# Seven of the sixteen blocks of an MLP's down projection by Strassen's seven products

## The chip, the core and the metric

The kernel runs on one core of one Trainium2 chip. The time is the device time of one launch in microseconds (us), the median of several runs. The engines have short names: PE is TensorE, ACT is ScalarE, DVE is VectorE, POOL is GpSimd and SP is SyncE, which issues the loads.

## What is computed

Two layers of a decoder trunk act on 256 tokens of width 1024 in float32. Each layer is a mixing part (attention, a recurrent branch and a pooling branch) and then an MLP. Only the MLP changes:

```python
h = h + RMSNorm_post(mix)
h = h + RMSNorm_post(SquaredReLU-MLP(RMSNorm_pre(h)))
```

The MLP's up projection is [256 x 1024] by [1024 x 4096], its hidden values are relu(.)^2, and its down projection is [256 x 4096] by [4096 x 1024].

## The kernel before

**A product in three matmuls.** Every float32 operand is split into two parts that TensorE takes as `float32r`: ACT copies the value rounded (the "hi", line 84) and DVE subtracts it from the original (the "lo", line 85). A product of two operands is then hi by hi, hi by lo and lo by hi, three matmuls that accumulate in one bank of PSUM (`mm3`, lines 91 to 94).

**The weights.** They come as 316 units of 128 x 1024 floats (512 KB), in the order in which they are used. SP issues one load for each (line 134) into one of 4 buffers named `raw`. ACT makes `wh` of it and DVE `wl`, into 8 buffers each. `take(n)` hands out the next n units, `split_to` and `ahead` issue copies and subtractions for units that come later, `load_to` issues loads. A raw buffer is free for the next load when DVE's subtraction has read it. The units on either side of a change of stage are split in two halves of 512 columns (`fine`).

**The MLP.** The 4096 hidden rows go in 8 chunks of 512. One *up unit* makes 256 hidden rows for all tokens: 48 matmuls of 256 columns into one bank (`w_unit`, line 276). Then ACT applies Relu out of the bank (line 731), squares (line 732) and copies the hi (line 84), and DVE subtracts the lo. The names in the profile are `z` for these values and `hid` for their two parts; `mh` and `ml` are the parts of the MLP's input. A chunk's share of the down projection is 48 matmuls of 512 columns (`s_hu`, line 289), which add to four banks: two halves of the tokens by two halves of the columns. All 8 chunks add to the same four banks (all banks are named `ps`). The loop, lines 745 to 750, puts the up units of the next chunk ahead of the down projection of this one. The first chunk (`up_first`, line 698) is computed with tokens as rows, since the second half of the tokens isn't normalised yet; eight transposes (line 706) turn it, one up unit later.

**The end of a layer.** The last two chunks' down projection goes half by half of the tokens (lines 750 to 770). After each half follows `residual` (line 253): ACT sums the squares of a bank (`junk`, line 229), DVE multiplies the bank by a gain (`yg`, line 264), DVE adds the two sums (line 233), ACT takes the root (line 245), DVE the reciprocal (line 246), and DVE adds to `h` (line 269). Then `mix_norm` does the same for the next layer's norm and scales (`un`, line 315), PE transposes (line 216), and ACT and DVE make `uh` and `ul` of the result (lines 222 and 224). The next layer's first products follow on PE (line 303). Both norm helpers are issued with a higher priority, so a scheduler moves them up on their engines. Each engine runs its own list of instructions in order.

Of the kernel before, what the change touches and what calls it, by code (L numbers as in the profile page):

```python
# [9 lines left out]
F32 = mybir.dt.float32  # L10
# [6 lines left out]
L = 2  # L17
D = 1024
# [16 lines left out]
FINE = (8, 8)  # L35
SQRT_2_PI = 0.7978845608028654
# [16 lines left out]
def trunk(ctx, tc, x, wts, rgw, par, gpost, eye, ctab, out):  # L53
    nc = tc.nc
    V, A, PE = nc.vector, nc.scalar, nc.tensor
# [23 lines left out]
    def bank(shape, nm="ps"):  # L79
        return psum.tile(shape, F32, tag="b", name=nm)  # L80
# [253 lines left out]
    for l in range(L):  # L334
# [358 lines left out]
        yb = [[bank([P, 512]) for _ in range(2)] for _ in range(2)]  # L693

        def new_hidden():
            return (acts.tile([P, 2, 4, T], F32R, tag="hi", name="hid"))

        def up_first():
            hus = take(4)
            hid = new_hidden()  # L700
            zs = []

            def hidden_T(tt):
                p2 = bank([P, 4, P])
                for j in range(4):
                    PE.transpose(p2[:, j, :], zs[tt][:, j * P:(j + 1) * P], ident)
                split(hid[:, 0, :, tt * P:(tt + 1) * P], hid[:, 1, :, tt * P:(tt + 1) * P], p2[:])

            for tt in range(2):
# [6 lines left out]
                z = ttile([P, 512], nm="z")  # L716
                A.activation(z[:], ps[:], AF.Relu)
                V.tensor_tensor(out=z[:], in0=z[:], in1=z[:], op=ALU.mult)
                zs.append(z)
            later(1, lambda: hidden_T(0))  # L720
            later(1, lambda: hidden_T(1))
            ahead()
            return hid

        def up(fc):
            hid = new_hidden()
            for u in range(2):
                ps = w_unit(take(2), uh, ul)
                tick()
                z = ttile([P, 2, T], nm="z")  # L730
                A.activation(z[:], ps[:], AF.Relu)
                A.activation(z[:], z[:], AF.Square)
                split(hid[:, 0, 2 * u:2 * u + 2, :], hid[:, 1, 2 * u:2 * u + 2, :], z[:])
                ahead()
            return hid

        def down(fc, hid):
            for nh in range(2):
                for i in range(2):
                    hu, = take(1)  # L740
                    for tt in range(2):
                        s_hu(yb[tt][nh][:], hu, hid[:, 0], hid[:, 1], 2 * i, tt, fc == 0 and i == 0, False)
                    ahead()

        hid = up_first()
        for fc in range(1, 7):
            nxt = up(fc)
            down(fc - 1, hid)
            hid = nxt
        hids = [hid, up(7)]  # L750
        hus = take(8)
# [3 lines left out]
        for tt in range(2):  # L755
            for f in range(2):
                for nh in range(2):
                    for i in range(2):
                        if tt == 1 and f == 1 and nh == 1 and i == 0 and l + 1 < L:
                            mix_features(0, un[0], l + 1)  # L760
                        s_hu(yb[tt][nh][:], hus[4 * f + 2 * nh + i], hids[f][:, 0], hids[f][:, 1], 2 * i, tt,
                             False, f == 1 and i == 1)
            residual(tt, yb[tt], msq[tt], gB)
# [43 lines left out]
def _layout(i):  # L807
    qc = np.concatenate([np.arange(hd * 64, hd * 64 + 64) for hd in _HEADS])
    units, rg, par, gp = [], [], [], []
    for l in range(L):  # L810
# [17 lines left out]
        up = _w_units(i["w_mlp_up"][l]).reshape(8, 4, P, HU_COLS)  # L828
        dn = _s_units(i["w_mlp_down"][l]).reshape(2, 8, 2, P, HU_COLS).transpose(1, 0, 2, 3, 4).reshape(8, 4, P, HU_COLS)
        units.append(up[0])  # L830
        for f in range(1, 8):
            units.append(up[f])
            units.append(dn[f - 1])
        units.append(dn[7])
# [34 lines left out]
```

## Time and profile before

| | |
|---|---|
| runs | 964.25, 965.38 and 965.0 us, median 965.0 |
| profiled execution | 964.16 us, its span 962.3 us, granted PE clock 0.999 |
| matmul instructions of PE | 5628, and 88 others in PE's row |
| loads of weight units | 316 of 512 KB |

The span runs from the first to the last instruction of the profiled execution; 1.9 us of its time lie around the span. A row of the timeline has the start in us, the duration of one instruction (or of a run of equal ones), engine, line and operation, then the tile written and the tiles read, the shape, and in brackets how long the engine was idle before it and what it waited for. On PE the matmuls are pipelined: one of 512 columns is shown as 0.39 us long, and the next one starts before it ends.

### The profile page before, as it was taken

The numbers are of one execution on the slowest core, as the hardware profiler recorded it, in microseconds if no ns is written. First come the engines' busy times: TensorE is split into PE (matmuls) and PEld (weight loads), VectorE is DVE, ScalarE is ACT, GpSimd is POOL, SyncE is SP. The second block draws the span as 40 slices with busy tenths as digits, with TensorE's granted clock in tenths as the row PEclk, the third lists the DMA queues.
The fourth block names the chain that finished last, engine by engine and source line by source line (L and its number), as shares of the span: only waits on it lengthen the run. The fifth ranks groups of instructions, "written<-read, shape, count | busy, mean of one in ns | idle before, by whom it ended". The sixth has DMA issues, their size and how long they took to land.

```text
span 962.3 us, 14953 instructions
## 1 busy us (share of the span) xinstructions
PE 951.3 (99%) x5716; PEld 835.3 (87%) x5716; DVE 649.7 (68%) x1101; ACT 599.8 (62%) x1001; POOL 2.6 (0%) x20
## 2 busy tenths in 40 slices
PE   8999999999999999999999999999999999999997
PEld 5898988988888999999888989888888899999995
DVE  6877886779768645445586778777897585545542
ACT  7754864789737655455566657566895476555541
POOL 0000000000000000000000000000000000000000
PEclk9999999999999999999999999999999999999999
DMA  7765456453755766665457536536358285665631
GB/s 277 244 205 185 132 166 195 161 178 111 254 161 176 226 192 192 183 192 176 134 183 257 172 111 210 179 103 219 124 178 262 88 276 179 195 185 188 185 122 44
DMA packets 48743, 173.28 MB, mean 180 GB/s; under 512 B 5408, under 2 KB 5792, under 8 KB 48672
## 3 DMA queue, kind: packets, MB, share of 16 engines
q1 hardware_dynamic: 48384, 172.16, 55.4%
q8 instruction: 45, 0.74, 0.3%
q14 instruction: 26, 0.21, 0.1%
q10 hardware_dynamic: 288, 0.17, 0.1%
HBM read 171.26 MB, written 1.05 MB: 179 GB/s over the span
## 4 chain that ended last, share of the span: by engine, by line
PE 97%; DMA 1%; ACT 1%; DVE 1%; issue 0%; SPq 0%; DVEq 0%; ACTq 0%
PE ps L92 28%; PE ps L93 28%; PE ps L94 28%; PE ps L303 8%; PE ps L391 1%; PE ps L439 1%; PE ps L428 1%; DMA raw<-wts 1%; PE ps L216 1%; PE ps L371 0%; PE ps L619 0%; ACT wh L84 0%; DVE h L269 0%; ACT junk L229 0%; DVE wl L85 0%
## 5 line engine op out<-in xcount | busy, mean ns | idle before, releaser
L85 DVE TENSOR_TENSOR wl<-raw,wh 128x1024 fp32r<-128x1024 f32 (+1 forms) x348 | 385.7, 1123 | 189.1 <-ACT wh L84 180.4
L84 ACT ACTIVATE wh<-raw 128x1024 fp32r<-128x1024 f32 (+1 forms) x348 | 334.2, 986 | 242.6 <-PE ps L94 106.2
L92 PE MATMUL ps<-mh,wh 128*128 128x256 f32 x448 | 126.9, 283 | 0.0
L94 PE MATMUL ps<-mh,wl 128*128 128x256 f32 x448 | 126.8, 283 | 0.0
L93 PE MATMUL ps<-ml,wh 128*128 128x256 f32 x448 | 126.8, 283 | 0.0
L92 PE MATMUL ps<-uh,wh 128*128 128x256 f32 x384 | 109.0, 284 | 0.0
L93 PE MATMUL ps<-ul,wh 128*128 128x256 f32 x384 | 108.7, 283 | 0.0
L94 PE MATMUL ps<-uh,wl 128*128 128x256 f32 x384 | 108.6, 283 | 0.0
L93 PE MATMUL ps<-wl,hid 128*128 128x512 f32 x256 | 99.9, 390 | 0.0
L92 PE MATMUL ps<-wh,hid 128*128 128x512 f32 x256 | 99.8, 390 | 0.0
L94 PE MATMUL ps<-wh,hid 128*128 128x512 f32 x256 | 99.6, 389 | 0.0
L92 PEld LDWEIGHTS ps<-mh,wh 128*128 128x128 f32 x448 | 86.0, 192 | 0.5
L93 PEld LDWEIGHTS ps<-ml,wh 128*128 128x128 f32 x448 | 85.9, 192 | 0.5
L94 PEld LDWEIGHTS ps<-mh,wl 128*128 128x128 f32 x448 | 86.0, 192 | 0.0
L92 PE MATMUL ps<-wh,uh 128*128 128x512 f32 x200 | 79.2, 396 | 0.7 <-ACT uh L222 0.7
L94 PE MATMUL ps<-wh,ul 128*128 128x512 f32 x200 | 78.1, 390 | 0.4 <-DVE ul L224 0.4
L93 PE MATMUL ps<-wl,uh 128*128 128x512 f32 x200 | 78.1, 390 | 0.0
L92 PEld LDWEIGHTS ps<-uh,wh 128*128 128x128 f32 x384 | 73.6, 192 | 1.1 <-issue 0.7
L93 PEld LDWEIGHTS ps<-ul,wh 128*128 128x128 f32 x384 | 73.6, 192 | 0.4
L94 PEld LDWEIGHTS ps<-uh,wl 128*128 128x128 f32 x384 | 73.6, 192 | 0.0
L94 PEld LDWEIGHTS ps<-wh,hid 128*128 128x128 f32 x256 | 48.1, 188 | 10.0
L92 PEld LDWEIGHTS ps<-wh,hid 128*128 128x128 f32 x256 | 48.1, 188 | 9.7
(190 smaller groups left out, 1589.8 us busy)
## 6 DMA issues: line engine op xcount, KB each, us to landing
raw<-wts SPq DMA_DIRECT2D x316, 512.0 KB, 4.3
gB<-gpost SPq DMA_DIRECT2D x4, 512.0 KB, 4.6
rg<-rgw SPq DMA_DIRECT2D x8, 256.0 KB, 3.9
out<-h SPq DMA_DIRECT2D x4, 256.0 KB, 2.1
h<-x SPq DMA_DIRECT2D x2, 256.0 KB, 3.3
h<-x SPq DMA_DIRECT2D x1, 512.0 KB, 7.0
cst<-ctab SPq DMA_DIRECT2D x1, 168.0 KB, 4.8
prm<-par ACTq DMA_DIRECT2D x1, 104.0 KB, 3.7
```

Of the source, the lines that this page charges most:

```text
L84: A.activation(hi, src, AF.Copy)
L85: V.tensor_tensor(out=lo, in0=src, in1=hi.bitcast(F32), op=ALU.subtract)
L92: PE.matmul(o, lh, rh, start=start, stop=False, **kw)
L93: PE.matmul(o, lh, rl, start=False, stop=False, **kw)
L94: PE.matmul(o, ll, rh, start=False, stop=stop, **kw)
L216: PE.transpose(banks[c // 4][:, c % 4, :], src[c // 4][:, (c % 4) * P:(c % 4 + 1) * P], ident)
L303: PE.matmul(o, xx[:, c, tsl], ww[c], start=(n == 0 and c == 0), stop=(n == 2 and c == 7))
L391: PE.matmul(sc[hd // hp][:, hd % hp, :], qT[a, j // 2][rows, j % 2, blk * P:(blk + 1) * P], kTs[0][rows, a, 0:w], start=True, stop=True)
L428: PE.transpose(ps[:, g, :], g8["p"](4 * b + g)[:, kt * P:(kt + 1) * P], ident)
L439: PE.matmul(ps[b * 64:b * 64 + 64, :, :], vt[kt][:, 256 + kv * 64:256 + kv * 64 + 64], g8[b, kt][:], start=(kt == 0), stop=(kt == nk - 1))
```

## The change

The hidden rows go in 16 blocks of 256, one up unit each. A block's share of the down projection is a product of a 2 x 2 arrangement of hidden blocks (128 tokens by 128 rows each) with a 2 x 2 arrangement of weight blocks (128 rows by 512 columns). In full it is 8 block products, 24 matmuls. For the first 7 blocks of each layer Strassen's method (in Winograd's form) takes 7 block products, 21 matmuls; the other 9 blocks stay in full ("plain") and come at the end. In numbers, 5628 matmuls become 5586.

In line numbers, a helper's line of before stands 6 lines further down in the change (84 is 90, 253 is 259). New are:
- `hidden_forms`: four sums of 128 x 128 hidden blocks on DVE (lines 746 to 749), and the splits of three blocks (384 columns) and of four sums (512 columns); the parts are named `xf`.
- `weight_sums`: of the two units of a block, one DVE sum of 1024 columns (line 763) and two of 512 (lines 767 and 768), named `wsum`, and the splits of a whole unit (`dh`, `dl`) and of half a unit (`bh`, `bl`). A raw buffer is free only when these sums, too, have read it.
- `weight_forms`: the splits of the sums (`sh`, `sl`), two of 1024 columns.
- `down`: 21 matmuls in a fixed order of products, into 7 banks named `pr`, which stay taken all through the stage. One of the 8 banks is left for the up units.
- The loop puts two up units beside each Strassen block: up unit, four products (12 matmuls), up unit, three products (9 matmuls). The last of the seven blocks has one up unit.
- After the Strassen blocks come 9 plain blocks of 24 matmuls, which go on adding to three of the product banks and one new one. The last three go half by half of the tokens. `drain` (lines 824 to 829) combines the other four product banks into SBUF behind the first plain block, and line 868 adds these to the banks ahead of `residual`, which then reads SBUF.
- `hidden_T` copies the transposed first units to `z` by four ACT copies (line 715), where before it split them.
- The units of the weights lie in another order: up units and Strassen pairs in turn, then the plain units.

```diff
+PLAIN = 9
+LAST = 3
+UPS = (2, 2, 2, 2, 2, 2, 1)
+NBLK = 16
...
-        yb = [[bank([P, 512]) for _ in range(2)] for _ in range(2)]
...
-                split(hid[:, 0, :, tt * P:(tt + 1) * P], hid[:, 1, :, tt * P:(tt + 1) * P], p2[:])
+                    PE.transpose(p2[:, j, :], toks[tt][:, j * P:(j + 1) * P], ident)
+                for j in range(2):
+                    A.activation(zs[j][:, :, tt * P:(tt + 1) * P], p2[:, 2 * j:2 * j + 2, :], AF.Copy)
...
+        def hidden_forms(j):
+            z = zs.pop(j)
+            a12, a22, a11, a21 = [z[:, i // 2, (i % 2) * P:(i % 2 + 1) * P] for i in range(4)]
+            sm = ttile([P, 4, P], nm="sm")
+            V.tensor_tensor(out=sm[:, 0, :], in0=a21, in1=a22, op=ALU.subtract)
+            V.tensor_tensor(out=sm[:, 2, :], in0=a11, in1=a21, op=ALU.subtract)
+            V.tensor_tensor(out=sm[:, 1, :], in0=sm[:, 0, :], in1=a11, op=ALU.subtract)
+            V.tensor_tensor(out=sm[:, 3, :], in0=a12, in1=sm[:, 1, :], op=ALU.add)
+            f = acts.tile([P, 2, 7, P], F32R, tag="hi", name="xf")
+            zf = z.rearrange("p c t -> p (c t)")[:, 0:384]
+            split(f[:, 0, 0:3, :].rearrange("p b t -> p (b t)"), f[:, 1, 0:3, :].rearrange("p b t -> p (b t)"), zf)
+            split(f[:, 0, 3:7, :], f[:, 1, 3:7, :], sm[:])
+            forms[j] = f
+        def weight_sums(j):
+            load_to(st["split"] + 2)
+            r0, r1 = raw_t.pop(st["split"]), raw_t.pop(st["split"] + 1)
+            st["split"] += 2
+            st["use"] += 2
+            t8 = acts.tile([P, 4, 512], F32, tag="lo", name="wsum")
+            V.tensor_tensor(out=t8[:, 0:2, :], in0=r0.rearrange("p (b n) -> p b n", b=2),
+                            in1=r1[:, 0:512].unsqueeze(1).to_broadcast([P, 2, 512]), op=ALU.add)
+            w1 = (his.tile([P, HU_COLS], F32R, tag="wh", name="dh"), los.tile([P, HU_COLS], F32R, tag="wl", name="dl"))
+            w4 = (ttile([P, 512], F32R, nm="bh"), ttile([P, 512], F32R, nm="bl"))
+            V.tensor_tensor(out=t8[:, 2, :], in0=t8[:, 0, :], in1=r0[:, 512:1024], op=ALU.add)
+            V.tensor_tensor(out=t8[:, 3, :], in0=t8[:, 2, :], in1=r1[:, 512:1024], op=ALU.add)
+            split(w1[0][:], w1[1][:], r0[:])
+            split(w4[0][:], w4[1][:], r1[:, 512:1024])
+            wforms[j] = [w1, w4, t8]
+            load_to(st["split"] + 3)
+        def weight_forms(j):
+            t8 = wforms[j].pop()
+            for i in range(2):
+                w = (his.tile([P, HU_COLS], F32R, tag="wh", name="sh"), los.tile([P, HU_COLS], F32R, tag="wl", name="sl"))
+                split(w[0][:], w[1][:], t8[:, 2 * i:2 * i + 2, :].rearrange("p b n -> p (b n)"))
+                wforms[j].append(w)
+        def down(j, part):
+            f = forms[j]
+            w1, w4, w2, w3 = wforms[j]
+            lo_, up_ = slice(0, 512), slice(512, 1024)
+            for p, blk, w, cs in ((1, 2, w1, up_), (3, 6, w1, lo_), (2, 0, w4, lo_), (7, 5, w2, lo_), (5, 3, w2, up_),
+                                  (6, 4, w3, lo_), (4, 1, w3, up_))[part]:
+                if p not in prods:
+                    prods[p] = bank([P, 512], nm="pr")
+                first, last = j == 0, j == nstr - 1 and p in (1, 5, 6, 7)
+                mm3(prods[p][:], f[:, 0, blk, :], f[:, 1, blk, :], w[0][:, cs], w[1][:, cs], first, last)
+        up_first()
+        split_to(st["use"] + 2)
+        up(2)
+        weight_sums(0)
+        split_to(st["use"] + 2)
+        weight_forms(0)
+        hidden_forms(0)
+        nup = 3
+        for j in range(nstr):
+            for i in range(UPS[j]):
+                up(nup)
+                nup += 1
+                if i == 0 and j + 1 < nstr:
+                    weight_sums(j + 1)
+                    hidden_forms(j + 1)
+                if nup < NBLK:
+                    split_to(st["use"] + 2)
+                down(j, slice(0, 7) if UPS[j] == 1 else (slice(0, 4), slice(4, 7))[i])
+            del forms[j], wforms[j]
+            if j + 1 < nstr:
+                weight_forms(j + 1)
...
+        def drain():
+            s1 = ttile([P, 512], nm="s1")
+            A.activation(s1[:], prods[1][:], AF.Copy)
+            u2, u3, u4, u5 = [ttile([P, 512], nm="us") for _ in range(4)]
+            V.tensor_tensor(out=u2[:], in0=prods[6][:], in1=s1[:], op=ALU.add)
+            V.tensor_tensor(out=u4[:], in0=prods[5][:], in1=u2[:], op=ALU.subtract)
+            V.tensor_tensor(out=u3[:], in0=prods[7][:], in1=u2[:], op=ALU.add)
+            V.tensor_tensor(out=u5[:], in0=prods[5][:], in1=u3[:], op=ALU.subtract)
+            return [[s1, u4], [u3, u5]]
+        def plain(j, hus, tt, nh):
+            for k in range(2):
+                wh, wl = hus[k]
+                cs, tsl = slice(nh * 512, (nh + 1) * 512), slice(tt * P, (tt + 1) * P)
+                mm3(tgt[tt][nh][:], hids[j][:, 0, k, tsl], hids[j][:, 1, k, tsl], wh[:, cs], wl[:, cs],
+                    tt == 1 and nh == 1 and j == nstr and k == 0, j == NBLK - 1 and k == 1)
...
+        tgt = [[prods[2], prods[3]], [prods[4], None]]
+        for j in range(nstr, NBLK - LAST):
+            if j not in hids:
+                hidden_split(j)
+            hus = take(2)
             ahead()
+            for tt in range(2):
+                for nh in range(2):
+                    if tgt[tt][nh] is None:
+                        tgt[tt][nh] = bank([P, 512], nm="pr")
+                    plain(j, hus, tt, nh)
+            if j == nstr:
+                rest = drain()
...
+        hus = take(2 * LAST)
...
+                for b in range(LAST):
+                    if tt == 1 and nh == 1 and b == LAST - 1 and l + 1 < L:
+                        mix_features(0, un[0], l + 1)
+                    plain(NBLK - LAST + b, hus[2 * b:2 * b + 2], tt, nh)
+            ys = [rest[tt][nh] for nh in range(2)]
+            for nh in range(2):
+                V.tensor_tensor(out=ys[nh][:], in0=tgt[tt][nh][:], in1=ys[nh][:], op=ALU.add)
+            residual(tt, ys, msq[tt], gB)
...
+        pairs = [np.stack([np.concatenate([d[c][:, 512:], d[1 - c][:, :512]], 1) for c in range(2)]) for d in dn]
+        units += [up[0], up[1], up[2], pairs[0], up[3]]
...
+        units += [dn[j] for j in range(nstr, NBLK)]
```
(`G` is named but not used. The dots leave out moved lines and code that is gone with the old loop.)

**What the engines' lists show: the start of the Strassen stage.** ACT, layer 0, before; numbers tell buffers apart, and `z_3432` is the second up unit's output:

```order
L84 ACTIVATE wh105_3549<-raw105_3515 128x1024
L84 ACTIVATE wh106_3567<-raw106_3517 128x1024
L84 ACTIVATE wh107_3585<-raw107_3535 128x1024
L84 ACTIVATE hid_3221<-ps_3418 128x4x128
L84 ACTIVATE hid_3221<-ps_3425 128x4x128
L731 ACTIVATE z_3432<-ps_3369 128x512
L732 ACTIVATE z_3432<-z_3432 128x512
L84 ACTIVATE hid_3368<-z_3432 128x512
L84 ACTIVATE wh108_3656<-raw108_3553 128x1024
L84 ACTIVATE wh109_3660<-raw109_3571 128x1024
```

The same stretch of ACT with the change, up to the last copy that block 0 needs (`xf_3472` from `sm_3467`):

```order
L90 ACTIVATE wh106_3555<-raw106_3457 128x1024
L715 ACTIVATE z_3217<-ps_3414 128x2x128
L715 ACTIVATE z_3218<-ps_3414 128x2x128
L715 ACTIVATE z_3217<-ps_3421 128x2x128
L715 ACTIVATE z_3218<-ps_3421 128x2x128
L735 ACTIVATE z_3428<-ps_3365 128x512
L90 ACTIVATE bh_3435<-raw101_3361 128x512
L736 ACTIVATE z_3428<-z_3428 128x512
L90 ACTIVATE xf_3472<-z_3217 128x384
L90 ACTIVATE xf_3550<-z_3218 128x384
L90 ACTIVATE wh107_3559<-raw107_3541 128x1024
L90 ACTIVATE xf_3472<-sm_3467 128x512
```

The copy of the hidden sums now stands behind `wh107`, a copy of a weight unit that is used later. DVE, with the change, at the same place:

```order
L767 TENSOR_TENSOR wsum_3529<-wsum_3529,raw104_3445 128x512
L91 TENSOR_TENSOR wl106_3556<-raw106_3457,wh106_3555 128x1024
L768 TENSOR_TENSOR wsum_3529<-wsum_3529,raw105_3455 128x512
L91 TENSOR_TENSOR bl_3436<-raw101_3361,bh_3435 128x512
L746 TENSOR_TENSOR sm_3467<-z_3217 128x128
L747 TENSOR_TENSOR sm_3467<-z_3217 128x128
L748 TENSOR_TENSOR sm_3467<-sm_3467,z_3217 128x128
L91 TENSOR_TENSOR xf_3472<-z_3217,xf_3472 128x384
L749 TENSOR_TENSOR sm_3467<-z_3217,sm_3467 128x128
L91 TENSOR_TENSOR xf_3550<-z_3218,xf_3550 128x384
L91 TENSOR_TENSOR wl107_3560<-raw107_3541,wh107_3559 128x1024
L91 TENSOR_TENSOR xf_3472<-sm_3467,xf_3472 128x512
```

The sums of block 1's weights (the last two are lines 767 and 768) stand ahead of block 0's hidden sums, and `wl107` ahead of the last subtraction for block 0.

**In the middle of the stage.** ACT, layer 0, before, at an up unit's Relu (line 731):

```order
L84 ACTIVATE hid_4226<-z_4276 128x512
L84 ACTIVATE wh140_4486<-raw140_4393 128x1024
L84 ACTIVATE wh141_4490<-raw141_4411 128x1024
L731 ACTIVATE z_4342<-ps_4293 128x512
L732 ACTIVATE z_4342<-z_4342 128x512
L84 ACTIVATE hid_4226<-z_4342 128x512
```

And with the change, between two Strassen blocks (Relu is line 735):

```order
L90 ACTIVATE sh_4049<-wsum_3922 128x1024
L90 ACTIVATE dh_4107<-raw122_3958 128x1024
L735 ACTIVATE z_4021<-ps_3972 128x512
L90 ACTIVATE wh124_4131<-raw124_4034 128x1024
L736 ACTIVATE z_4021<-z_4021 128x512
L90 ACTIVATE xf_4126<-z_3642 128x384
L90 ACTIVATE wh125_4135<-raw125_4117 128x1024
L90 ACTIVATE wh126_4207<-raw126_4119 128x1024
L90 ACTIVATE wh127_4211<-raw127_4139 128x1024
```

Two copies for the next block, `sh` and `dh`, stand ahead of the Relu, and the hidden split stands behind one more weight copy.

**The end of layer 0.** DVE, before, from the reciprocal for the first half of the tokens to that half's `un`:

```order
L246 RECIPROCAL s_4867<-s_4866 128x1
L85 TENSOR_TENSOR wl158_4994<-raw158_4799,wh158_4993 128x512
L269 SCALAR_TENSOR_TENSOR h_82<-yg_4858,s_4867,h_82 128x512
L269 SCALAR_TENSOR_TENSOR h_82<-yg_4862,s_4867,h_82 128x512
L85 TENSOR_TENSOR wl159_5000<-raw159_4801,wh159_4999 128x512 x2
L85 TENSOR_TENSOR wl160_5012<-raw160_4803,wh160_5011 128x512
L233 TENSOR_TENSOR s_4877<-s_4872 128x1
L85 TENSOR_TENSOR wl160_5012<-raw160_4803,wh160_5011 128x512
L85 TENSOR_TENSOR wl161_5018<-raw161_5005,wh161_5017 128x512
L246 RECIPROCAL s_4880<-s_4879 128x1
L85 TENSOR_TENSOR wl161_5018<-raw161_5005,wh161_5017 128x512
L315 TENSOR_SCALAR un_4883<-h_82,s_4880 128x512
```

And with the change, to the same row (`us` and `s1` are drained sums):

```order
L868 TENSOR_TENSOR us_4733<-pr_3571,us_4733 128x512
L270 SCALAR_TENSOR_TENSOR yg_5008<-us_4733,s_3640,gB2_3199 128x512
L239 TENSOR_TENSOR s_5010<-s_5001 128x1
L252 RECIPROCAL s_5013<-s_5012 128x1
L275 SCALAR_TENSOR_TENSOR h_82<-yg_5004,s_5013,h_82 128x512
L275 SCALAR_TENSOR_TENSOR h_82<-yg_5008,s_5013,h_82 128x512
L868 TENSOR_TENSOR us_4732<-pr_3665,us_4732 128x512
L239 TENSOR_TENSOR s_5023<-s_5018 128x1
L91 TENSOR_TENSOR wl160_5148<-raw160_4959,wh160_5147 128x512
L252 RECIPROCAL s_5026<-s_5025 128x1
L91 TENSOR_TENSOR wl160_5148<-raw160_4959,wh160_5147 128x512
L321 TENSOR_SCALAR un_5029<-h_82,s_5026 128x512
```

The additions of line 868 come in; the second half's (`us_4732`) stands ahead of the first half's `un`. Two subtractions for the next layer's weights lie in the stretch, where seven did. On PE, 40 matmuls of the second half lie ahead of the first half's eight transposes and 8 behind them before; with the change 33 and 3.

More of the change, by code (lines that the diff above doesn't have):

```diff
@@ L737, in down, with up @@
[L737 to L751, printed above, removed]
+        def up(j):
+            ps = w_unit(take(2), uh, ul)
+            tick()
+            z = ttile([P, 2, T], nm="z")
+            A.activation(z[:], ps[:], AF.Relu)
+            A.activation(z[:], z[:], AF.Square)
+            zs[j] = z
@@ L752, in trunk @@
+        for j in range(NBLK - LAST, NBLK):
+            if j not in hids:
+                hidden_split(j)
+        hus = take(2 * LAST)
         un = []
```

62 lines of the change are left out of this document (27 added, 35 removed).

## The prediction

> **What bounds the kernel now.** I read the page's first two parts first, then the chain that ended last, then the costliest groups.
>
> ```profile
> PE 951.3 (99%) x5716; PEld 835.3 (87%) x5716; DVE 649.7 (68%) x1101; ACT 599.8 (62%) x1001; POOL 2.6 (0%) x20
> ...
> PEclk9999999999999999999999999999999999999999
> ...
> PE 97%; DMA 1%; ACT 1%; DVE 1%; issue 0%; SPq 0%; DVEq 0%; ACTq 0%
> ...
> L93 PE MATMUL ps<-wl,hid 128*128 128x512 f32 x256 | 99.9, 390 | 0.0
> ```
>
> TensorE is busy for 99% of the span at full clock, 97% of the chain is its work, and its matmuls of the down projection wait for nothing (0.0). So a matmul that goes away shortens the span, as long as no wait replaces it. The 390 ns of a row is not what one is worth: they overlap. The worth is the distance between starts. Here are one of the first and the last of 48 in one block of the down projection, then the first matmul of the up units and the first behind them:
>
> ```profile
> 439.70 0.39 PE L94 MATMUL ps<-wh,hid 128*128 128x512 f32 x1
> ...
> 449.22 0.39 PE L94 MATMUL ps<-wh,hid 128*128 128x512 f32 x1
> 449.44 0.28 PE L92 MATMUL ps<-mh,wh 128*128 128x256 f32 x1
> ...
> 460.96 0.40 PE L92 MATMUL ps<-wh,hid 128*128 128x512 f32 x1
> ```
>
> Between the first two lie 42 starts: 9.52 / 42 = **0.2267 us** for a matmul of 512 columns. From 449.44 to 460.96 are two up units, 96 matmuls: **0.120 us** each, 5.76 us a unit.
>
> **The removed work.** Seven blocks in each of two layers lose three matmuls: 7 x 3 x 2 = 42, all of 512 columns. 42 x 0.2267 = **-9.5 us**. By the 390 ns of the row it would be 16.4 us, which I don't believe.
>
> **The added work on VectorE and ACT.** It costs only where PE must wait for it. These are the two engines in the MLP before, in a window of 160 us and in its groups:
>
> ```profile
> 322.00:482.00 160.00, 159.99 (x1000) 144.87 (x998) 83.01 (x93) 89.25 (x124) 0.00 (x0) 1.00 0.59 179
> ```
> ```profile
> L85 DVE TENSOR_TENSOR wl<-raw,wh 128x1024 fp32r<-128x1024 f32 x51 | 62.5, 1226 | 60.6 <-ACT wh L84 60.6
> ...
> L84 ACT ACTIVATE wh<-raw 128x1024 fp32r<-128x1024 f32 x50 | 53.0, 1061 | 61.6 <-PE ps L93 32.6 <-PE ps L94 29.0
> ...
> L85 DVE TENSOR_TENSOR hid<-z,hid 128x512 fp32r<-128x512 f32 x14 | 9.7, 693 | 6.8 <-ACT hid L84 6.8
> L732 ACT ACTIVATE z<-z 128x512 f32<-128x512 f32 x14 | 8.8, 631 | 0.4
> ...
> L731 ACT ACTIVATE z<-ps 128x512 f32<-128x512 f32 x14 | 8.1, 579 | 0.0
> ```
> ```profile
> 496.50 0.29 DVE L344 TENSOR_TENSOR rt<-qkv,cst 128x128 f32<-128x128 f32 x1 [0.27 <-ACT qkv L361]
> ```
>
> The window shows DVE busy for 83 of 160 us and ACT for 89. In the Strassen stage a period is two up units and 21 matmuls: 2 x 5.76 + 21 x 0.2267 = 16.28 us. DVE then has seven subtractions of 1024 columns (four `wl`, one `dl`, two `sl`): 7 x 1.226 = 8.58. The sum of 1024 columns I price like them, 1.23; that it reads one operand twice is in no row, so its bounds are 1.23 and twice that. Two sums and two subtractions of 512 columns are 4 x 0.69 = 2.76, four sums of 128 columns 4 x 0.29 = 1.16, and the subtraction of 384 columns about 0.56, between 0.29 and 0.69. Sum **14.3 us of 16.28**, 88%. ACT has 7 x 1.061 + 0.62 + 0.5 + 0.63 + 2 x (0.58 + 0.63) = 11.6 us, 71%. The loads are six units in 16.28 us where before were eight in 22.4, 193 against 187 GB/s. Nothing is over its period, so I take **0** for the steady stage.
>
> In the plain stage a block has 24 matmuls, 5.44 us, beside two copies and one hidden split on ACT (2 x 1.06 + 0.63 = 2.75) and as many subtractions on DVE (3.14): 0. The drain's sums lie behind the first plain block on DVE; four of about 0.69 (the row of an operation on a bank under the tail) fit into its slack: 0.
>
> **The one free bank.** Seven banks hold products, so an up unit can start only when Relu has emptied the bank of the unit before. Before, a Relu behind one weight copy ran like this:
>
> ```profile
> 343.18 1.06 ACT L84 ACTIVATE wh<-raw 128x1024 fp32r<-128x1024 f32 x1 [0.38 <-PE ps L93]
> 344.14 0.58 ACT L731 ACTIVATE z<-ps 128x512 f32<-128x512 f32 x1
> ```
>
> That unit ended at about 343.1: the last unit ahead of it ends at 326.4 (next part), and 48 x 0.2267 and 48 x 0.120 follow. So the bank was free 1.6 us after the unit, at 344.7. With the change nine matmuls lie between a unit and the next, 9 x 0.2267 = 2.04 us, or twelve, 2.72. The cover lasts with 0.4 us to spare: **0**, with a copy of 1.06 more ahead as the upper bound (the first rival).
>
> **The start of the Strassen stage** is where I expect a wait. Layer 0 before:
>
> ```profile
> 307.99 2.16 DVE L224 SCALAR_TENSOR_TENSOR ml<-ps,prm,mh 128x128 fp32r<-128x128 f32 x8
> ...
> 313.36 2.48 DVE L85 TENSOR_TENSOR wl<-raw,wh 128x1024 fp32r<-128x1024 f32 x2 [0.28 <-ACT wh L84]
> ...
> 314.86 0.60 ACT L717 ACTIVATE z<-ps 128x512 f32<-128x512 f32 x1 [0.28 <-PE ps L303]
> ...
> 320.61 0.36 PE L92 MATMUL ps<-mh,wh 128*128 128x256 f32 x1
> ```
> ```profile
> DMA to landing us min/median/max: 3.4/4.5/6.0
> ```
>
> (The last row is that of the weight loads issued from 300 to 340 us.) PE's order up to there is that of before, so its first product comes after the unit that starts at 320.6: 320.6 + 48 x 0.120 = 326.4. (The Relu at 314.86 gives the last tokens' values, which DVE squares and PE transposes just ahead of that unit, so they are no part of the wait.) The third product needs the hi of the hidden sums, three matmuls after that, at 327.1. On ACT that copy stands behind `wh107`. The load of `raw107` takes the buffer of `raw104`, which is free only when DVE has made the second sum of block 1 (line 767). DVE is free of `ml` at 310.1 and then has, in its order, up to that sum: the first `dl` and the sums of block 0 (1.23 + 1.23 + 2 x 0.69), two `wl`, two `sl`, the sum and the `dl` of block 1 (six of 1.23) and two of 0.69 (the squares of the first tokens and the sum itself). That is 12.6 us of work and, I estimate, 0.2 us of waiting for ACT, whose copies of the same stretch run ahead of it: **322.9**. The load lands 3.4 to 4.5 us later, 326.3 to 327.4; `wh107` and the hidden copy take 1.06 + 0.63, so the copy is there at 328.0 to 329.1, 0.9 to 2.0 us after 327.1. Its lo comes 0.6 us after on DVE. So 1.5 to 2.6 us are lost, and I take 1.8; the second layer has the same order, so **+3.6 us**. Bounds: 0, if DVE's chain is 2 us shorter than I add it up, and 3.9 a layer with a landing of 6.0.
>
> **The end of layer 0.**
>
> ```profile
> 480.47 0.88 DVE L315 TENSOR_SCALAR un<-h,s 128x512 f32<-128x512 f32 x2
> ...
> 482.17 2.15 ACT L222 ACTIVATE uh<-ps,prm 128x128 fp32r<-128x128 f32 x8
> ```
> ```profile
> PE ps L216 <- DVE un L315: 1.6, 2, 0.8
> ```
>
> Before, PE waited twice for `un`, 1.6 us. For the first half of the tokens `un` was ready at 481.3. Only 33 matmuls (7.5 us) now cover the chain from its last product to `un`, not 40 (9.1). But that chain had seven subtractions for later weights in it and has two now (-5 x 0.63), and gains an addition of 0.69: I take -0.3. For the second half 3 matmuls and not 8 lie behind the transposes, so 5 x 0.2267 = 1.1 us of cover go from its chain and from the eight `uh` copies (2.15 us); I take +0.8, and +0.4 for copies of the next weights that ACT makes later. Together **+0.9**; bounds -0.3 and +2.
>
> **The tail of the kernel.**
>
> ```profile
> 956.38 0.75 DVE L264 SCALAR_TENSOR_TENSOR yg<-ps,s,gB 128x512 f32<-128x512 f32 x1 [1.97 <-ACT junk L229]
> ```
> ```profile
> 290.10 0.69 DVE L262 TENSOR_TENSOR yg<-ps,gB 128x512 f32<-128x512 f32 x1 [2.03 <-ACT junk L229]
> ```
>
> An addition (0.69) comes in ahead of the last squares. Before, the gain multiply waited for the squares of the same bank (`junk`, line 229); with the sum in SBUF both can run side by side. **+0.1**; bounds -0.1 and +0.7.
>
> **The sum.** -9.5 + 0 + 0 + 3.6 + 0.9 + 0.1 = -4.9. The profiled execution took 964.16 us (span 962.3 and 1.9 around it), which gives 959.3; it lies 0.8 below the median of 965.0, so on that footing **960.0**.
>
> **The rivals.**
>
> 1. *The free bank comes late* (the slower side). ACT's Relu stands behind `sh` and `dh`, and `sh` waits for DVE's sums. If DVE runs late, or one copy and one hidden split (1.06 + 0.63) come ahead of a Relu, the bank is 1.69 - 0.4 = 1.3 us late in each of the 12 periods with nine matmuls of cover: +15 us, 975. Half of it gives 968. It loses to before from 0.4 us of lateness a period on (4.9 / 12). For it: a split of 1024 more columns is queued per period than before. Against it: 29% of ACT's period is free. 0.08.
> 2. *VectorE becomes the bound.* If the sum that reads an operand twice takes 2.45 and the two sums of 512 columns 1.4 each, a period is 14.3 + 1.2 + 1.4 = 16.9, 0.6 over, x 12 = 7.6: 968. It decides from 16.7 us a period. For it: 88% by rows. Against: each price is from the nearest row. 0.05.
> 3. *No wait at the start.* If `raw107` lands before it is needed, the 3.6 us don't come: 956.4. For it: ACT's copies can be earlier than I place them. 0.15.
> 4. *The late load takes 6.0 us:* 3.9 a layer, 964. 0.06. [...]
> 5. *The clock falters.* [...] 0.02.
> 6. *A matmul is worth its 390 ns:* 953. 0.02.
>
> **How the numbers follow.** The forecast has 0.62. The range is **955.0 to 966.5**: it takes in rivals 3 and 4 and the bounds of the start and of the layer's end, and leaves out 5, 6 and most of 1 and 2. A measurement of this kernel tells 0.2% (1.9 us) from no change. Faster: the forecast but for its upper tail (0.62, less 0.02), rival 3 (0.15), 6 (0.02) and a little of 1 and 2 (0.02): **0.79**. The same: the tail and rival 4, 0.02 + 0.05 + 0.02 of 1 and 2: **0.09**. Slower: the rest of 1, 2, 4 and 5: **0.12**.
>
> **What would show it.** 42 matmuls fewer on PE and starts 0.227 us apart in the Strassen stage; PE idle for 1 to 3 us at block 0's products (line 98), waiting for `xf`, once in each layer, and nowhere else in the stage; no up unit waiting for Relu (line 735); DVE busy for about 14.3 of each 16.3 us there; PE's wait for `un` about 1 us longer; PEclk 9 throughout. I am wrong if an up unit waits for its bank in each period, if DVE is busy without a gap there, or if block 0 starts without a wait.

## The result, and the profile after

The changed kernel takes **961.86 us** (median of 7 runs, 960.43 to 963.03), the kernel before 965.0 (963.95 to 965.77): a ratio of **0.9967**, 95% interval 0.9956 to 0.9979. It is 3.1 us faster; forecast were 5.0. The profiled execution took 960.85 us, its span is 959.1, 3.2 shorter than before.

The page of the changed kernel, the rows that answer to those of before:

```profile
PE 946.3 (99%) x5674; PEld 827.5 (86%) x5674; DVE 730.0 (76%) x1253; ACT 620.5 (65%) x1049; POOL 2.6 (0%) x20
...
PEclk9999999999999999999999999999999999999999
...
PE 88%; DMA 5%; DVE 4%; ACT 1%; issue 1%; DVEq 0%; SPq 0%; ACTq 0%
...
L98 PE MATMUL pr<-wh,hid 128*128 128x512 f32 x144 | 56.1, 390 | 0.0
```

PE has 42 instructions fewer, and VectorE is busy for 80 us more. The clock holds (0.996 over the span). But the chain that ended last is now only 88% PE, and 5% of it are loads of weight units. So something waits for loads. What PE waited for, in the view of waits (us in total, times, longest; the rows left out stand for the kernel's first 17 us and, with 0.5 us, for a step ahead of the MLP):

```profile
PE ps L98 <- ACT z L735: 1.3, 2, 1.0
...
PE pr L100 <- DVE xf L91: 0.6, 2, 0.3
...
PE ps L309 <- DVE ml L230: 0.4, 1, 0.4
```

The first row is new: an up unit that waits for Relu, twice. The second, block 0 waiting for its hidden sums, was forecast. The third, products of the MLP's input, is new as well. These figures are too small for what is lost, though. A matmul is shown as 0.39 us long while the next may start after 0.227, so a wait of less than 0.16 us doesn't show at all and a longer one shows 0.16 too short. A loss on PE is read from the distance between starts. Four places that both kernels have, on the timeline of PE; first before:

```profile
319.82 1.03 PE L706 MATMUL ps<-idt,z 128*128 128x128 f32 x8
...
492.25 1.04 PE L216 MATMUL ps<-idt,un 128*128 128x128 f32 x8
...
792.43 1.03 PE L706 MATMUL ps<-idt,z 128*128 128x128 f32 x8
...
955.14 0.39 PE L94 MATMUL ps<-wh,hid 128*128 128x512 f32 x1
```

and the same places after:

```profile
320.38 1.03 PE L713 MATMUL ps<-idt,zt 128*128 128x128 f32 x8
...
489.90 1.09 PE L222 MATMUL ps<-idt,un 128*128 128x128 f32 x8
...
792.43 1.04 PE L713 MATMUL ps<-idt,zt 128*128 128x128 f32 x8
...
951.81 0.39 PE L100 MATMUL pr<-wh,hid 128*128 128x512 f32 x1
```

| stretch | its length, after against before | matmuls moved or gone | lost |
|---|---|---|---|
| start to layer 0's first up unit | +0.56 | 0 | 0.6 |
| to the second half's transposes at the layer's end | -2.91 | 27 (6 of them now lie behind it): -6.13 | 3.2 |
| to layer 1's first up unit | +2.35 | the 6: +1.36 | 1.0 |
| to the last matmul | -3.33 | 21: -4.77 | 1.4 |
| the rest of the span | +0.13 | 0 | 0.1 |

The losses are 6.3 us, the 42 matmuls 9.5, and the difference is the 3.2 us of the span. So the matmuls paid in full, at 0.227 us each, and the question is where the 6.3 us lie.

**Block 0** (forecast 1.8 a layer). The weight copy that waits for its load, the hidden copy behind it, VectorE's subtraction for the same weight unit, the one for the hidden sums behind it, and PE's matmul that waits for that; ACT, DVE and PE in turn:

```profile
325.93 1.06 ACT L90 ACTIVATE wh<-raw 128x1024 fp32r<-128x1024 f32 x1 [0.66 <-DMA raw<-wts]
326.89 0.62 ACT L90 ACTIVATE xf<-sm 128x512 fp32r<-128x512 f32 x1
```
```profile
327.02 1.23 DVE L91 TENSOR_TENSOR wl<-raw,wh 128x1024 fp32r<-128x1024 f32 x1 [0.48 <-ACT wh L90]
328.16 0.69 DVE L91 TENSOR_TENSOR xf<-sm,xf 128x512 fp32r<-128x512 f32 x1
```
```profile
328.16 0.40 PE L98 MATMUL pr<-bh,xf 128*128 128x512 f32 x1
328.90 0.50 PE L100 MATMUL pr<-dh,xf 128*128 128x512 f32 x1 [0.34 <-DVE xf L91]
329.24 0.39 PE L99 MATMUL pr<-bl,xf 128*128 128x512 f32 x1
```

From 328.16 to 329.24 are two starts in 1.08 us, where 0.45 would do: 0.6 lost, and 0.5 in the second layer.

**The second up unit of the third Strassen block** (forecast 0; the expectations below call it the third up unit). Its bank is emptied by a Relu that stands behind a weight copy, which waits for a load:

```profile
362.58 1.06 ACT L90 ACTIVATE wh<-raw 128x1024 fp32r<-128x1024 f32 x1 [1.57 <-DMA raw<-wts]
363.55 0.58 ACT L735 ACTIVATE z<-ps 128x512 f32<-128x512 f32 x1
```
```profile
362.81 0.39 PE L100 MATMUL pr<-sh,xf 128*128 128x512 f32 x1
364.18 0.39 PE L98 MATMUL ps<-mh,wh 128*128 128x256 f32 x1 [0.98 <-ACT z L735]
```

1.37 us from start to start, 1.14 lost; 0.46 at the same place of the second layer.

**The end of layer 0** (forecast +0.9). PE's first products of the next layer, before and after:

```profile
483.86 1.98 PE L303 MATMUL ps<-wh,uh 128*128 128x512 f32 x8
...
487.48 1.98 PE L303 MATMUL ps<-wl,uh 128*128 128x512 f32 x8
```
```profile
481.69 2.07 PE L309 MATMUL ps<-wh,uh 128*128 128x512 f32 x8
...
487.55 1.99 PE L309 MATMUL ps<-wl,uh 128*128 128x512 f32 x8
```

Before, 16 starts take 3.62 us, 0.226 each. After, 21 starts take 5.86 us, where 4.77 would do: 1.1 lost. PE loads one operand of each matmul by an instruction of its own (`PEld` in the profile; the page has 5674 of each), and its waits show for what:

```profile
486.22 0.19 PEld L309 LDWEIGHTS ps<-wh,uh 128*128 128x128 f32 x1 [0.33 <-ACT wh L90]
...
486.69 0.70 PEld L309 LDWEIGHTS ps<-wh,ul 128*128 128x128 f32 x3 [0.29 <-DVE ul L230]
```

In this stretch four such waits end with a weight copy (0.9 us in all) and two with a piece of `ul` (0.6 us).

**Layer 1's MLP input** (not forecast). VectorE makes `ml` behind the first sum for block 0, and that sum waits for a load; on DVE, then PE:

```profile
779.67 1.23 DVE L763 TENSOR_TENSOR wsum<-raw,raw 128x1024 f32<-128x1024 f32 x1 [1.31 <-DMA raw<-wts]
780.82 2.15 DVE L230 SCALAR_TENSOR_TENSOR ml<-ps,prm,mh 128x128 fp32r<-128x128 f32 x8
```
```profile
781.22 1.42 PE L309 MATMUL ps<-wh,ml 128*128 128x256 f32 x5 [0.35 <-DVE ml L230]
```

PE's matmuls there follow `ml`'s pieces 0.26 us apart instead of 0.12: about 1.0 lost.

Block 0, the bank and the end of layer 0 make up 2.8 of the 3.2 us of the table's second row; block 0 and the bank of layer 1 make up 1.0 of the 1.4 us of its fourth. The other 0.4 us in each are spread out, with no more than 0.1 us at any one place.

The 0.6 us ahead of layer 0's first up unit are in part none of the change's: 0.4 of them lie in the first 48 us, where the program is the same, and the windows show a granted clock of 0.91 in the first 20 us of this execution against 1.00 before.

### The profile page after: what moved, and what is told of

It is laid out like the page before. It is cut to its first block, busy times and chain, and to the rows that moved or that the text cites. A ratio compares the mean times of both kernels' runs of the same rounds, so it can differ in the third digit from the quotient of the medians.

```text
span 959.1 us, 15057 instructions
## 1 busy us (share of the span) xinstructions
PE 946.3 (99%) x5674; PEld 827.5 (86%) x5674; DVE 730.0 (76%) x1253; ACT 620.5 (65%) x1049; POOL 2.6 (0%) x20
## 4 chain that ended last, share of the span: by engine, by line
PE 88%; DMA 5%; DVE 4%; ACT 1%; issue 1%; DVEq 0%; SPq 0%; ACTq 0%
PE ps L98 20%; PE ps L100 20%; PE ps L99 20%; PE ps L309 7%; DMA raw<-wts 5%; PE pr L100 5%; PE pr L99 5%; PE pr L98 5%; PE ps L397 1%; PE ps L445 1%; DVE wl L91 1%; PE ps L434 1%; ACT wh L90 1%; PE ps L222 0%; PE ps L377 0%
## 5 line engine op out<-in xcount | busy, mean ns | idle before, releaser
L91 DVE TENSOR_TENSOR wl<-raw,wh 128x1024 fp32r<-128x1024 f32 (+1 forms) x316 | 349.8, 1126 | 121.4 <-ACT wh L90 113.8
L90 ACT ACTIVATE wh<-raw 128x1024 fp32r<-128x1024 f32 (+1 forms) x316 | 302.2, 987 | 192.7 <-PE ps L100 60.2
L98 PE MATMUL pr<-wh,hid 128*128 128x512 f32 x144 | 56.1, 390 | 0.0
L100 PE MATMUL pr<-wh,hid 128*128 128x512 f32 x144 | 56.0, 389 | 0.0
L99 PE MATMUL pr<-wl,hid 128*128 128x512 f32 x144 | 56.0, 389 | 0.0
L98 PEld LDWEIGHTS ps<-wh,uh 128*128 128x128 f32 x200 | 37.9, 189 | 11.1 <-issue 2.3
L100 PEld LDWEIGHTS ps<-wh,ul 128*128 128x128 f32 x200 | 37.9, 189 | 8.9 <-DVE ul L230 0.8
```

The costliest lines, as they stand in the source:

```text
L90: A.activation(hi, src, AF.Copy)
L91: V.tensor_tensor(out=lo, in0=src, in1=hi.bitcast(F32), op=ALU.subtract)
L98: PE.matmul(o, lh, rh, start=start, stop=False, **kw)
L99: PE.matmul(o, lh, rl, start=False, stop=False, **kw)
L100: PE.matmul(o, ll, rh, start=False, stop=stop, **kw)
```

## The experiments

Times are medians, with the ratio to the kernel before on the same chip (its medians there were 964.2 to 964.6) and its 95% interval. Beside the changed kernel it was 965.0, so a difference to the changed kernel is uncertain by some 0.5 us. Edits are against the changed kernel.

**Four Strassen blocks.** Is a block a gain, and what are the fixed costs?

```diff
-PLAIN = 9
+PLAIN = 12
-UPS = (2, 2, 2, 2, 2, 2, 1)
+UPS = (2, 2, 2, 1)
...
+        while nup < NBLK:
+            up(nup)
+            nup += 1
+            if nup < NBLK:
+                split_to(st["use"] + 2)
```

> Four Strassen blocks in each layer in place of seven (12 plain blocks; the up units left over run between the two stages). Theory A: a block's three matmuls are a clear gain, and what is lost is lost at fixed places (the start of the stage, the third up unit's bank, the ends of the stages). Then 3 x 3 x 2 = 18 matmuls come back, 18 x 0.227 = +4.1 us on the changed kernel's 961.9: about 966, and the lost time at the fixed places stays. Rival B: each block's sums and splits cost about what its matmuls save, so the time hardly moves: 961 to 963.

Measured: **972.45 us** (1.0091, 1.0076 to 1.0107). Neither theory gives that. The up units that are left over run one behind the other, and the one bank stops them. PE, then ACT:

```profile
386.82 0.28 PE L100 MATMUL ps<-mh,wl 128*128 128x256 f32 x1
388.62 0.39 PE L98 MATMUL ps<-mh,wh 128*128 128x256 f32 x1 [1.51 <-ACT z L735]
```
```profile
387.99 0.58 ACT L735 ACTIVATE z<-ps 128x512 f32<-128x512 f32 x1
```

1.80 us from start to start instead of 0.12, and 0.1 more behind it: 1.77 lost, at two places in each layer, 7.1 us. Without them the kernel is 3.5 us above the change, near the 4.1 of theory A, though the runs spread from 970.8 to 976.0. The run didn't settle the question it was made for, but it prices the bank: with no matmuls as cover, one up unit behind another costs 1.8 us.

**Relu twice.** How thin is the cover of the one bank?

```diff
             A.activation(z[:], ps[:], AF.Relu)
+            A.activation(z[:], ps[:], AF.Relu)
             A.activation(z[:], z[:], AF.Square)
```

> The Relu that empties the up unit's bank is issued twice in a row, so the bank is free about 0.5 us later in every period. Theory A: the one free bank is covered with 0.44 us to spare where nine matmuls lie between two units and with 0.1 to 0.5 where twelve do, so PE waits now in most periods, about 2.2 us a layer: +4 to +5 us on 961.9, 966 to 967, with waits of up units for line 735. Rival B: there is slack on ACT that takes it up: below +1 us.

Measured: **964.59 us** (1.0003, 0.9993 to 1.0013), +2.7 on the change. The waits of its profile:

```profile
PE ps L98 <- ACT z L736: 4.9, 4, 2.2
```

Nearer to A than to B, but not in most periods: five units lose 0.1 to 2.4 us by their starts, the rest nothing. With the second Relu the scheduler also put more matmuls between some units (9 to 14, where it was 9 and 12), so the edit thickened the cover while it raised the cost.

**The sum twice.** Is VectorE the bound?

```diff
             V.tensor_tensor(out=t8[:, 0:2, :], in0=r0.rearrange("p (b n) -> p b n", b=2),
                             in1=r1[:, 0:512].unsqueeze(1).to_broadcast([P, 2, 512]), op=ALU.add)
+            V.tensor_tensor(out=t8[:, 0:2, :], in0=r0.rearrange("p (b n) -> p b n", b=2),
+                            in1=r1[:, 0:512].unsqueeze(1).to_broadcast([P, 2, 512]), op=ALU.add)
```

> The sum of 1024 columns on VectorE is issued twice for each block: VectorE has 15.5 us of work instead of 14.3 in a period of 16.3. Theory A: VectorE is not the bound of the steady stage; only at the stage's start, where the load waits for its sums, PE waits about 1 to 2 us longer in each layer: +1 to +4 us, 963 to 966, nothing in later periods. Rival B: VectorE bounds the stage: 13 periods by 1.1 us, about +14 us, 976.

Measured: **963.34 us** (0.9988, 0.9979 to 0.9997), +1.5. B falls. A holds in size and not in place:

```profile
PE ps L98 <- ACT z L735: 5.5, 4, 1.9
```

The wait grew at the bank, to 5.5 us in four periods from 1.3 in two; at block 0 it is gone. My explanation is that a late VectorE reaches PE through the raw buffers: later sums, later loads, later copies, and Relu behind them. This run doesn't show the steps one by one.

**Five raw buffers.** Do the waits come from the loads?

```diff
-NRAW = 4
-NTMP = 28
+NRAW = 5
+NTMP = 26
```

> Five raw buffers for weight units in place of four (26 temporary tiles instead of 28, to make room). Theory A: the waits at block 0's products (0.6 and 0.5 us), at the third up unit's bank (1.2 and 0.6 us) and for the MLP input's lo in the second layer (about 1.0 us) all come from a unit's load that is issued late because its raw buffer is freed late. Then most of these 3.9 us go: 958 to 960. Rival B: they come from the order of the copies on ACT and the sums on VectorE, whatever the loads do: 961 to 963.

Measured: **960.47 us** (0.9948, 0.9935 to 0.9960). Its waits:

```profile
PE ps L309 <- ACT mh L228: 1.8, 2, 1.5
...
```

The rows left out lie in the kernel's first 15 us. No matmul waits for block 0 (`xf`) or for Relu any more, in either layer. At the bank the order on ACT is that of the change, and the copy ahead of Relu no longer waits for its load:

```profile
359.90 1.06 ACT L90 ACTIVATE wh<-raw 128x1024 fp32r<-128x1024 f32 x1 [0.38 <-PE ps L99]
360.87 0.58 ACT L735 ACTIVATE z<-ps 128x512 f32<-128x512 f32 x1
```

So that wait came from a late load, as A says. At block 0 the order changed too: the hidden copy now stands ahead of the weight copy that it stood behind.

```profile
325.85 0.63 ACT L90 ACTIVATE xf<-sm 128x512 fp32r<-128x512 f32 x1 [0.70 <-DVE sm L749]
```

There the run doesn't tell the earlier load from the other order. And the MLP's start got worse, so there A is wrong. ACT in layer 1:

```profile
778.18 1.06 ACT L90 ACTIVATE wh<-raw 128x1024 fp32r<-128x1024 f32 x1 [3.97 <-DMA raw<-wts]
779.14 2.16 ACT L228 ACTIVATE mh<-ps,prm 128x128 fp32r<-128x128 f32 x8
```

A copy for later now stands ahead of the MLP input's hi and waits 4.0 us for its load; PE's longest wait for `mh` is 1.5 us. More buffers changed the order on ACT, and what the order puts ahead of a critical step is what costs.

**The MLP's input first.** One element of block 0's first sum (VectorE), and of its weight copy (ACT), is written first from the MLP input's parts, then overwritten:

```diff
+            if j == 0:
+                V.tensor_scalar(t8[:, 0, 0:1], uls[:, 7, T - 1:T].bitcast(F32), 1.0, None, op0=ALU.mult)
             V.tensor_tensor(out=t8[:, 0:2, :], in0=r0.rearrange("p (b n) -> p b n", b=2),
...
+            if j == 0:
+                A.activation(w1[0][:, 0:1], uhs[:, 7, T - 1:T], AF.Copy)
```

> One element of block 0's first weight sum, and one of its weight copy, is written first from the MLP input's parts, so that VectorE and ACT can only start on block 0's weights behind the splits of the MLP input. Theory A: the wait of the second layer's first MLP products (about 1.0 us) came from these weight operations standing ahead of the splits and waiting for a load; it goes, while block 0's products wait as before or up to 1 us longer: 960.5 to 962. Rival B: the splits are late for another reason (the residual ahead of them), the wait stays and the time is 962 to 963.

Measured: **958.52 us** (0.9938, 0.9924 to 0.9952), 3.3 less than the change, more than A gave. On DVE in layer 1 nothing waits for a load ahead of `ml` now:

```profile
777.12 2.16 DVE L230 SCALAR_TENSOR_TENSOR ml<-ps,prm,mh 128x128 fp32r<-128x128 f32 x8 [0.72 <-ACT mh L228]
```

From the start of the normalised input's transposes to layer 1's first up unit PE takes 1.3 us less. Block 0's wait went too, which I had not expected of it; the waits for Relu stay (2.6 us in three).

**The last blocks one by one.**

```diff
-            for nh in range(2):
-                for b in range(LAST):
+            for nh, b in [(n, b) for n in range(2) for b in range(LAST)] if tt == 0 else [(n, b) for b in range(LAST) for n in range(2)]:
```

> In the second half of the tokens the last three blocks are taken block by block (both halves of the columns of a block in a row), where the change takes all blocks for one half of the columns and then for the other; so two blocks' weight buffers are free 12 and 24 matmuls into the half and not only in its last 12. Theory A: the 0.75 us that PE loses at the first products of the next layer come from weight copies that are late because the buffers are held: they go, 961.1. Rival B: they come from ACT's and VectorE's work for the norm there, and the shorter way from a bank's last product to the sums costs more: 962 to 963.

Measured: **959.73 us** (0.9951, 0.9938 to 0.9965), 2.1 less than the change. PE's first products of the next layer:

```profile
479.79 3.20 PE L309 MATMUL ps<-wh,uh 128*128 128x512 f32 x12
...
486.56 1.76 PE L309 MATMUL ps<-wl,uh 128*128 128x512 f32 x7
```

28 starts in 6.77 us, 0.4 lost instead of 1.1, and no weight load of PE waits for a weight copy there any more: theory A, for 0.7 us at this place. While PE works on the last three blocks ACT now makes eight copies of half units ahead of the first `uh`, where it made five. The other 1.4 us of the difference of medians are not shown to come from it: a wait for Relu is as large as ever in its profile (1.9 us), and the runs of both kernels spread over 2.6 and 3.7 us.

**The three mends together.** The last three edits in one kernel.

> Five raw buffers, block 0's weights behind the splits of the MLP input, and the last blocks block by block, together. Theory A: the three losses are apart from one another. Five buffers alone gave 960.5 with 4.7 us more waiting than before at the two starts of the MLP; these and the 0.75 us at the layer's end go: 955 to 956. Rival B: with the splits ahead, block 0's weights come late and PE waits there for what it gains: 959 to 960.

Measured: **953.69 us** (0.9888, 0.9874 to 0.9902), a little below A; 8.2 us less than the change, 10.7 less than before on the same chip. The waits that the profile shows are of the kinds that it showed before the change, and all of them lie in the kernel's first 15 us:

```profile
PE ps L222 <- DVE un L321: 2.0, 2, 1.3
PE ps L126 <- DVE warm L123: 1.2, 1, 1.2
PE ps L98 <- ACT uh L228: 0.5, 1, 0.5
PE ps L100 <- DVE ul L230: 0.4, 1, 0.4
```

The four runs lie within 0.6 us (953.46 to 954.06), where those of the changed kernel spread over 2.6. That its waits for loads make this spread is not shown: the seven runs of the kernel before, measured beside it, spread over 1.8 us.

**Eight, ten and twelve blocks with the mends.** Does VectorE become the bound? The three edits, and the numbers at the top:

```diff
-PLAIN = 9
+PLAIN = 8
-UPS = (2, 2, 2, 2, 2, 2, 1)
+UPS = (2, 2, 2, 2, 2, 1, 1, 1)
```

> The three mends and an eighth Strassen block in each layer, with one up unit beside each of the last three Strassen blocks. Theory A: a block beside one up unit is not free, since its period is 5.76 + 21 x 0.227 = 10.5 us and VectorE has 14.3 - 2 x 1.23 = 11.8 us of work in it: up to 1.3 us are lost in each of three periods in two layers against the 1.4 us saved, so 0 to +5 us on the kernel with the mends. Rival B: earlier slack takes it up, -1.4 us on it.

Measured: **952.25 us** (0.9872, 0.9856 to 0.9888): -1.44, theory B. With ten, `PLAIN = 6` and `UPS = (2, 2, 2, 1, 1, 1, 1, 1, 1, 1)`:

> The three mends and ten Strassen blocks in each layer, seven of them beside one up unit. Theory A: each further block is worth its matmuls as long as the sums are done ahead, as the eighth was: two more than in the kernel with eight, 2 x 3 x 2 x 0.227 = 2.7 us less, 949.5, no waits. Rival B: VectorE has 11.8 us of work in a period of 10.5 with one up unit; seven of these in a row put it 7 x 1.3 = 9 us behind, less the two or three periods of work it has done ahead: PE waits for several us in the last blocks of each layer, and the time is 953 to 965.

Measured: **950.32 us** (0.9850, 0.9833 to 0.9866), theory A within a microsecond, but not its "no waits": in layer 1 PE waits twice for `xf` (0.3 and 0.2 us in the view of waits, 0.8 by the starts, near 894 us), the kind of wait that rival B names, but far smaller. With twelve, `PLAIN = 4` and `UPS` one 2 and eleven 1:

> The three mends and twelve Strassen blocks in each layer, eleven of them beside one up unit. Theory A (no bound by VectorE): four blocks more than eight, 5.4 us less, 946.8. Rival B (VectorE is the bound of a period with one up unit, 11.8 against 10.5 us): up to 11 x 1.3 x 2 = 29 us lost against the 5.4 saved, less what is done ahead: 955 to 975, with PE waiting for xf or for the sums' splits in each late period and VectorE busy without a gap.

Measured: **947.21 us** (0.9821, 0.9806 to 0.9836), theory A, and the fastest kernel of all, 17 us below the kernel before. VectorE *is* nearly at its limit there, busy for 59.2 of 60 us in a window of the stage, and PE waits for nothing:

```profile
340.00:400.00 60.00, 60.00 (x389) 54.84 (x388) 59.19 (x86) 43.92 (x57) 0.00 (x0) 1.00 0.60 194
```

(Columns: length, then busy time of PE, PE's loads, DVE, ACT and POOL, then clock, DMA share and GB/s.) Why it doesn't stop PE is seen on DVE's timeline, the same instruction (`dl`) of two blocks in a row, and two subtractions between them:

```profile
379.07 1.22 DVE L91 TENSOR_TENSOR dl<-raw,dh 128x1024 fp32r<-128x1024 f32 x1
...
381.27 2.35 DVE L91 TENSOR_TENSOR wl<-raw,wh 128x1024 fp32r<-128x1024 f32 x2
...
389.82 1.23 DVE L91 TENSOR_TENSOR dl<-raw,dh 128x1024 fp32r<-128x1024 f32 x1
```

A block takes VectorE 10.75 us, and 0.17 of these are a wait for a load. It is not the 11.8 that I had added up from durations, since the instructions that follow one another here overlap: two of 1.22 us are done in 2.35. PE's products of two blocks in a row start 10.56 us apart on average. So VectorE falls about 0.2 us behind a block. The work done ahead covers it: in layer 0 its subtraction for a block's hidden sums starts 4.2 us ahead of PE's first product of that block at the third block, and 2.5 us ahead at the eleventh.

**Twelve blocks without the mends.** The last two numbers alone, all else as in the change.

> Twelve Strassen blocks in each layer and none of the three mends (four raw buffers, the change's order at the MLP's start and at its end). Theory A: the mends and the further blocks add up, so this is the changed kernel less five blocks' matmuls, 961.9 - 30 x 0.227 = 955. Rival B: the mends are what makes the further blocks free; with four raw buffers each period with one up unit adds waits for loads, and 958 to 965 comes out.

Measured: **950.71 us** (0.9854, 0.9838 to 0.9870), below both. Its profile has no wait for Relu at all (the first row lies in the kernel's first 10 us):

```profile
PE ps L98 <- ACT uh L228: 1.7, 1, 1.7
...
PE pr L100 <- DVE xf L91: 0.8, 2, 0.4
```

With one up unit to a block, all 21 matmuls (4.8 us) lie between two units, and a Relu behind a copy that waits for a load is still in time. So in this profile the further blocks also take the thin place away; by the medians the mends are worth 3.5 us with twelve blocks and 8.2 with seven.

## Why the prediction was right, and where its sum was not

- **The removed work: right.** 42 matmuls, 0.227 us each between starts; the stretches add up with that price, and eight, ten and twelve blocks follow it (6.5 us for five blocks, 6.8 by the price).
- **VectorE is not the bound: right, with wrong prices.** 14.3 us of a period of 16.3 was added up from durations. In the changed kernel VectorE was busy for 80.5 of the 100 us from 330 to 430, 13.1 of 16.3. In the row without gaps of the kernel with twelve blocks the instructions start closer together than they are long (two of 1.22 us in 2.35), and a block with one up unit took 10.75 us where durations say 11.8.
- **The start of the stage: the mechanism right, the size not.** The term +3.6 measured 1.1 (0.6 and 0.5). The load landed at 325.9 and not 326.3 to 327.4, and PE came 0.6 us later than I had it. Two errors more work against each other. The lo was made 1.3 us after the hi and not 0.6, since VectorE's subtraction of the weight unit stands between; and PE had three matmuls (0.7 us) to do that need no lo. (It is the second product that needs the hidden sums, not the third; the 327.1 is the second's.)
- **The one free bank: the step that failed.** "The cover lasts with 0.4 us to spare: 0" took the Relu behind one copy that is ready. In the changed kernel a copy ahead of it can wait for its load, and 1.14 and 0.46 us were lost at one unit of each layer. It is the first rival's place with another cause: not a copy more, but a copy that waits. Five raw buffers took it away, with the same order on ACT.
- **The end of layer 0: the sum right, its parts not.** +0.9 was forecast and about 1 us was lost. The second half's `un`, forecast +0.8, cost PE 0.1. The copies of the next weights, forecast +0.4, were most of it, with pieces of `ul` for the rest, and both stand behind work for the second half's norm (`junk` on ACT, `h` on VectorE). Freeing the buffers of the last blocks earlier brought 0.7 of it back. The wait for `un` that I quoted (1.6 us in two) isn't from there: on PE's timeline both lie in the kernel's first 14 us. A row of totals has no place; I should have looked for it.
- **Layer 1's MLP input: missing in the prediction**, 1.0 us. I followed VectorE's list from `ml` on and did not look at what stands ahead of `ml`.
- **The tail: right** (+0.1 forecast, +0.13 measured): on the timeline the gain multiply and the squares both start at 952.96, right behind the addition.
- **The clock held.** No run shows the clock fall in the MLP; the 0.02 of the fifth rival rests on such a fall, and so does the 0.01 of the fourth that the prediction counts as slower (0.06 less 0.05). The mean granted clock of every execution, of all kernels, lies between 0.994 and 0.999. From 20 us to the end of the changed kernel's span the granted clock is 1.00, and so it is in the window of the kernel with twelve blocks, where PE is busy for 60.00 of 60 us. PE's longest wait in the changed kernel's MLP was 1.14 us, not the 3.9 of the fourth rival.

Forecast losses were 4.6 us and measured ones 6.3. That the time came within 2 us of the forecast is in part luck: the start of the stage was put 2.5 us too high, and the bank (1.6 us) and layer 1's MLP input (1.0 us), both put at nothing, make up for it.

## What to carry to other kernels

On a kernel that one engine bounds, price removed and added work by the distance between starts, and then look for the losses not in the engines' totals but in their lists: at each step that the bound engine waits for, which instruction stands ahead of it, and what does that one wait for. A weight copy that waits for a load, ahead of the operation that empties the only free bank, cost 1.14 us here, as much as five of the saved matmuls at 0.227 us each. And when a stage is short of cover, more of the saving work can be the cure: one up unit to a Strassen block left 4.8 us of cover where two left 2.0, and with twelve blocks and none of the mends no matmul waited for Relu.

## What was not expected of the hardware

- In the kernel with twelve blocks VectorE's instructions that followed each other without waiting overlapped, by 0.09 us at 1024 columns (2 x 1.22 against 2.35); over a block, without its wait for a load, that was 1.2 of 11.8 us.
- Loads of equal size (512 KB) landed at very different times after their issue: 3.4 to 6.9 us for 42 weight units of the changed kernel (320 to 430 us), 4.3 in the median. Whether this makes the 2.6 us between its runs isn't shown.
